# Tying the first running sum of each accumulator of the later modulations to its place in the source

## The chip, the cores and the metric

The kernel runs on one core of one Trainium2 chip. The metric is device time in microseconds (us), the median of repeated executions; lower is better. The engines are named as in the profile: PE (TensorE), DVE (VectorE), ACT (ScalarE), POOL (GpSimd) and SP, the engine that issues nearly all transfers (DMAs) from one queue, in the order in which they stand there.

## The reference

One layer of a streaming encoder: a prompt of 2048 tokens and a sample of 64, of width 1024. Scale, shift and gate of both halves of the layer come from the conditioning vectors c through one matrix, the six "modulations" of 1024 values each:

```python
def mlstm_chunk(carry, xs):
    C, n, m = carry
    q, k, v, ig, lf = xs
    ...
    a = wt * jnp.einsum('bhtd,bhsd->bhts', q, k)
    num = jnp.einsum('bhts,bhsd->bhtd', a, v) + g_inter[..., None] * jnp.einsum('bhvk,bhtk->bhtv', C, q)
```

The first half normalises x, projects it to a pooling mixer and to four heads of an mLSTM (queries, keys, values, gates; a matrix memory C carried from chunk to chunk), and projects back with a gated residual. The second half is a gated MLP of width 2816 with a causal convolution of width 3, again with a gated residual. All results are float32.

## The kernel before

The 2112 tokens are taken in four groups: 512, 512, 512 and 576. For each group the attention half runs on PE in this order: the projection of values and gates (`L1083`), then for each head the projections q, k, o (`L423`), between whose matmuls the head's mLSTM is laid (`L1173` to `L1265`), then pooling and the output projection. The MLP follows for all groups in stretches of hand-set order.

Weights. The matmuls of `L423` read units of 512 KB, `wt<-hl_kept` (`L355`), 12 matmuls to a unit (24 in the last group), two units to a projection. Six buffers hold units, and a unit's load is issued once PE has read the unit that held its buffer.

Gate chain. Between the gate projection and the first head stands a chain of some ten DVE and ACT steps on tiles of 4 rows, `L1118` to `L1186`: two scans (`L1136`, `L1144`), `R` (`L1159`, `L1161`) and `RHL` (`L1164`), which PE needs at `L1173` and `L1219`. `CL` and `GL` come from them; `kw` (`L1233`), `at` (`L1225`, `L1244`), the state updates `st` (`L1258`) and `nd` (`L1267`) are the mLSTM's own DVE steps.

Background work runs in generators which the main loop advances a step at a time:

- `ada(m, first)` makes modulation m, one per group (m = 2 in the first, then 3, 4, 5). It reads 16 blocks of `w_ada` of 128 x 512 (256 KB, `L188`), eight to each of two halves, into `raw` tiles, of which there are four (`RB`; m = 2 uses other tiles). For each block DVE adds to two accumulators: `tensor_scalar` at `L201` begins a half (k = 0), `scalar_tensor_tensor` at `L203` goes on (k = 1 to 7), each with the block times a column of `CA`, the conditioning. Three loads are issued ahead; the next one is issued behind the sums that free a buffer. Sums over partitions on PE (`L211`), a copy, transposes and the bias (`L221`) end it.
- `up_sums` loads `w_up` (`L843`), works on it on DVE (`L864` to `L868`) and stores `wsum` (`L853`) for the MLP; its steps keep the order of the source.
- The norm of the second half, in the last group, loads `mx<-x2d` (`L710`), works on DVE (`L698`) and ACT, stores `h2d` (`L718`).

The order on each engine is set by a tile scheduler, outside the hand-set stretches of the MLP: it may place an instruction earlier or later than the source has it, as long as data and buffers allow. `tc.keep_in_program_order(ins)` takes that freedom away for one instruction: it stays behind the instruction that stands ahead of it in the source on the same engine. It adds no semaphore and no work. Of all DMAs from SP at most eight are under way.

Of the kernel before, what the change touches and what calls it, by code (L numbers as in the profile page):

```python
# [12 lines left out]
ALU = mybir.AluOpType  # L13
# [46 lines left out]
def tile_layer(ctx: ExitStack, tc: tile.TileContext, xT, vecs, cst, rst, rowv, w_mod, w_ada, w_qkou, w_v, w_pool,  # L60
               w_out, w_up, w_down, st_C, st_pool, yT, o_pool, o_C, o_m, o_conv):
    nc = tc.nc
    act, dve, pool, pe = nc.scalar, nc.vector, nc.gpsimd, nc.tensor
# [19 lines left out]
    def m2_ps():  # L83
        return bank("m2")
# [9 lines left out]
    def scr():  # L94
        return sp.tile([P, TMAX], F32, tag="scr", name="scr")
# [56 lines left out]
    CA = cp.tile([P, KD, 2], F32, tag="CA", name="CA")  # L152
# [6 lines left out]
    def raw_tile():  # L159
        return wp.tile([P, WN], F32, tag="raw", name="raw", bufs=RB)  # L160
# [10 lines left out]
    def ada(m, first):  # L171


        todo = [(j, k) for j in range(2) for k in range(KD)]
        src = [w_ada[m - 2, k, :, j * 512:(j + 1) * 512] for j, k in todo]
        got = {}

        def load(i):
            if first:

                if i % 2 == 0 and i < len(todo):
                    w = a1.tile([P, 4, 256], F32, tag="w4", name="w4", bufs=5).rearrange("p (a b) c -> p a (b c)", a=2)
                    for d in range(2):
                        got[i + d] = w[:, d]
                        tc.keep_in_program_order(nc.sync.dma_start(out=w[:, d], in_=src[i + d]))
            elif i < len(todo):
                got[i] = raw_tile()[:, :512]
                nc.sync.dma_start(out=got[i], in_=src[i])  # L188
        lead = 4 if first else 3
        for i in range(lead):  # L190
            load(i)
        yield
        accs = []
        for i, (j, k) in enumerate(todo):
            if k == 0:
                acc = [a1.tile([P, 512], F32, tag="acc", name="acc", bufs=4) for _ in range(2)]
                accs += acc
            w = got.pop(i)
            for s in range(2):
                if k == 0:  # L200
                    dve.tensor_scalar(out=acc[s], in0=w, scalar1=CA[:, k, s:s + 1], scalar2=None, op0=ALU.mult)  # L201
                else:
                    dve.scalar_tensor_tensor(out=acc[s], in0=w, scalar=CA[:, k, s:s + 1], in1=acc[s],  # L203
                                             op0=ALU.mult, op1=ALU.add)
            load(i + lead)
            yield
        yield

        pt = m2_ps()
        for c, acc in enumerate(accs):  # L210
            pe.matmul(pt[32 * c:32 * c + 32, :], ones[:, 0:32], acc, start=True, stop=True)  # L211
        MR = scr()
        dve.tensor_copy(MR[:, :512], pt)
        yield
        yield
        pt = m2_ps()
        for n in range(4):
            pe.transpose(pt[:, n * P:(n + 1) * P], MR[:, n * P:(n + 1) * P], ident)
        for j in range(2):
            bia = V[:, V_BA + m * 8 + 4 * j:V_BA + m * 8 + 4 * j + 4]  # L220
            dve.tensor_tensor(out=MOD[:, m, 4 * j:4 * j + 4],  # L221
                              in0=pt.rearrange("p (n c t) -> p n c t", n=4, c=4)[:, :, 2 * j:2 * j + 2, 0],
                              in1=bia.unsqueeze(2).broadcast_to([P, 4, 2]), op=ALU.add)
        if m == 4:
            scale_cols(G2, V_G2, 4, 0, KD)
        yield

    def scale_cols(G, v0, m, k0, n):
        dve.scalar_tensor_tensor(out=G[:, k0:k0 + n], in0=MOD[:, m, k0:k0 + n], scalar=1.0,
                                 in1=V[:, v0 + k0:v0 + k0 + n].unsqueeze(2).broadcast_to([P, n, 2]),  # L230
                                 op0=ALU.add, op1=ALU.mult)
# [101 lines left out]
    class Unit:  # L333

        state = 0
        w = raw = None
# [494 lines left out]
    if True:  # L831
# [536 lines left out]
        for o in groups:  # L1368
# [3 lines left out]
            if o.g > 0:  # L1372
                bg[3].append(ada(2 + o.g, False))
                tick(3)
# [18 lines left out]
            if o.g == 0:  # L1393
                bg[3].append(ada(2, True))
# [505 lines left out]
```

## Time and profile before

| | |
|---|---|
| time, median of 3 runs | 2216.25 us (2215.57 to 2217.02) |
| the profiled execution | 2218.49 us |
| its span | 2216.7 us |
| mean granted PE clock | 0.995 |
| PE busy | 2191.5 us, 99% |
| DVE busy | 1570.1 us, 71% |
| ACT busy | 1004.3 us, 45% |
| DMA, whole span | 498.58 MB, 225 GB/s |

In the rows of the profile, `out<-in` are the program's names, `xcount` counts instructions that stand together, and a bracket holds the idle time before a row and what ended it. `SPq` is SP's queue of issues. The attention half ends near 806 us; groups 1, 2 and 3 begin their first head near 238, 424 and 613 us. The numbers behind names, as in `wt_4568`, tell tiles apart; where the profile leaves them out, the n-th issue of a kind in the trace is the n-th of its kind in the order.

### The profile page before, as it was taken

To read this page: it belongs to the slowest core of one execution; us is meant where nothing else is said; L and a number is where in the kernel's file an instruction comes from. 1 tells how busy PE (TensorE), PEld (TensorE's weight loads), DVE (VectorE), ACT (ScalarE), POOL (GpSimd) and SP (SyncE) were. 2 spreads that over 40 slices of the span, in tenths; PEclk is the share of its full clock that TensorE was granted. 3 is DMA by queue.
4 is the path that set the end of the run, shared out by engine and by line. 5 is a ranking of instruction groups with operands and counts; after the bars stand their busy time and mean duration, and the time that the engine had idled before them with its cause. 6 is when DMAs were issued, how large, how long until landed. Compare 5 with 4: busy or idle time off the path is not lost.

```text
span 2216.7 us, 38129 instructions
## 1 busy us (share of the span) xinstructions
PE 2191.5 (99%) x13798; PEld 2081.8 (94%) x13798; DVE 1570.1 (71%) x2917; ACT 1004.3 (45%) x1992; POOL 203.2 (9%) x481
## 2 busy tenths in 40 slices
PE   8999999999999999999999999999999999999998
PEld 6888888888899999999999999999999999999998
DVE  4877659577765768687858687777767685767474
ACT  3553334234343446464636454545445353445354
POOL 0010000001000100010100210000001210101012
PEclk9999999999999999999999999999999999999999
DMA  9978987997898695757656876556458565353442
GB/s 352 339 241 269 337 280 239 320 318 244 286 326 273 215 307 176 231 170 262 201 179 223 279 225 204 181 193 203 152 163 283 187 193 161 111 177 120 149 150 80
DMA packets 279357, 498.58 MB, mean 225 GB/s; under 512 B 25176, under 2 KB 105432, under 8 KB 279168
## 3 DMA queue, kind: packets, MB, share of 16 engines
q1 hardware_dynamic: 267392, 468.05, 64.6%
q10 hardware_dynamic: 11776, 28.09, 3.4%
q8 instruction: 109, 1.79, 0.3%
q14 instruction: 80, 0.66, 0.1%
HBM read 385.29 MB, written 110.75 MB: 224 GB/s over the span
## 4 chain that ended last, share of the span: by engine, by line
PE 91%; DMA 4%; DVE 2%; ACT 1%; issue 1%; SPq 1%; POOL 0%; POOLq 0%; DVEq 0%; ACTq 0%
PE mm L1488 37%; PE mm L423 23%; PE mm L1751 21%; PE mm L1083 3%; DMA wt<-wsum 1%; DMA raw<-w_down 1%; PE mm L1013 1%; PE m L1264 1%; PE m L1265 1%; DMA wt<-hl_kept 1%; PE m L1242 1%; PE m L1253 1%; PE m L1345 1%; PE p L1013 1%; DMA mx<-x2d 1%
## 5 line engine op out<-in xcount | busy, mean ns | idle before, releaser
L1488 PE MATMUL mm<-hx,wt 128*128 128x352 f32 x5544 | 886.1, 321 | 2.5 <-DVE ea L1540 2.4
L1488 PEld LDWEIGHTS mm<-hx,wt 128*128 128x128 f32 x5544 | 879.6, 188 | 4.5 <-ACT wt L366 2.5
L1751 PE MATMUL mm<-av,wt 128*128 128x352 f32 (+2 forms) x3168 | 509.7, 321 | 0.7 <-DVE av L1611 0.3
L1751 PEld LDWEIGHTS mm<-av,wt 128*128 128x128 f32 x3168 | 502.6, 188 | 4.2 <-ACT av L1603 1.2
L423 PE MATMUL mm<-hl,wt 128*128 128x512 f32 (+2 forms) x1920 | 397.6, 358 | 3.9 <-DMA wt<-hl_kept 2.7
L369 DVE TENSOR_TENSOR wt<-raw,wt 128x512 fp32r<-128x512 f32 (+3 forms) x494 | 307.1, 637 | 93.1 <-ACT wt L366 92.0
L366 ACT ACTIVATE wt<-raw 128x512 fp32r<-128x512 f32 (+3 forms) x494 | 271.7, 570 | 213.6 <-PE mm L1751 83.6
L423 PEld LDWEIGHTS mm<-hl,wt 128*128 128x128 f32 x1920 | 312.4, 188 | 52.1 <-issue 5.1
L1766 DVE SCALAR_TENSOR_TENSOR x<-mm,MOD,x 128x352 f32<-128x352 f32 (+4 forms) x224 | 106.5, 526 | 114.7 <-PE mm L1751 114.6
L423 PE MATMUL mm<-mx,wt 128*128 128x512 f32 (+1 forms) x960 | 186.7, 353 | 0.0
L423 PEld LDWEIGHTS mm<-mx,wt 128*128 128x128 f32 x960 | 158.7, 188 | 25.3 <-ACT mx L1347 1.1
L1476 DVE SCALAR_TENSOR_TENSOR tg<-eg,V,tg 128x704 f32<-128x704 f32 (+1 forms) x132 | 125.7, 952 | 47.9 <-ACT tg L1471 45.5
L369 DVE TENSOR_TENSOR wt<-wt 128x512 fp32r<-128x512 f32 x176 | 121.8, 693 | 53.1 <-ACT wt L366 52.7
L366 ACT ACTIVATE wt<-wt 128x512 fp32r<-128x512 f32 x176 | 110.2, 627 | 85.9 <-DMA wt<-wsum 74.3
L1476 DVE SCALAR_TENSOR_TENSOR ta<-ea,V,ta 128x704 f32<-128x704 f32 (+1 forms) x132 | 125.6, 952 | 8.5 <-ACT ta L1471 5.9
L1611 DVE TENSOR_TENSOR av<-tg,av 128x704 fp32r<-128x704 f32 (+4 forms) x112 | 62.1, 589 | 42.5 <-ACT av L1603 42.3
L1582 ACT ACTIVATE tg<-tg 128x704 f32<-128x704 f32 (+1 forms) x66 | 52.4, 794 | 77.7 <-DVE tg L1476 77.7
L1496 DVE TENSOR_TENSOR eg<-mm,u 128x352 f32<-128x352 f32 x154 | 70.2, 468 | 20.6 <-ACT u L1551 11.2
L203 DVE SCALAR_TENSOR_TENSOR acc<-raw,CA,acc 128x512 f32<-128x512 f32 x84 | 60.6, 748 | 32.7 <-DMA raw<-w_ada 32.6
L1536 ACT ACTIVATE u<-mm 128x352 f32<-128x352 f32 x66 | 30.4, 461 | 115.2 <-PE mm L1488 74.5
L1083 PE MATMUL mm<-wt,hl 128*128 128x256 f32 (+1 forms) x576 | 70.9, 282 | 0.0
L1083 PEld LDWEIGHTS mm<-wt,hl 128*128 128x128 f32 x576 | 69.2, 188 | 1.0 <-issue 0.6
(294 smaller groups left out, 1958.9 us busy)
## 6 DMA issues: line engine op xcount, KB each, us to landing
wt<-hl_kept SPq DMA_DIRECT2D x108, 512.0 KB, 5.9
raw<-w_up SPq DMA_DIRECT2D x198, 256.0 KB, 3.6
wt<-wsum SPq DMA_DIRECT2D x176, 256.0 KB, 4.1
wt<-wsplit SPq DMA_DIRECT2D x88, 512.0 KB, 4.1
raw<-w_down SPq DMA_DIRECT2D x96, 256.0 KB, 2.9
w<-w_up SPq DMA_DIRECT2D x88, 256.0 KB, 5.8
wsum<-w SPq DMA_DIRECT2D x44, 512.0 KB, 6.3
wsplit<-wt SPq DMA_DIRECT2D x44, 512.0 KB, 4.4
```

The source lines that it names most:

```text
L203: dve.scalar_tensor_tensor(out=acc[s], in0=w, scalar=CA[:, k, s:s + 1], in1=acc[s], op0=ALU.mult, op1=ALU.add)
L366: act.activation(u.w[:, 0, :u.n], u.raw[:, :u.n], AF.Copy)
L369: dve.tensor_tensor(out=u.w[:, 1, :u.n], in0=u.raw[:, :u.n], in1=u.w[:, 0, :u.n].bitcast(F32), op=ALU.subtract)
L423: pe.matmul(ps[bi][:, :hi - lo], U[:, a, k % 4 * P:(k % 4 + 1) * P], mv[k][:, b, lo:hi], start=(at == 0 and pi == 0), stop=(k == order[-1] ...
L1083: pe.matmul(ps[ti][:n, :cols], h[4 * kh + k4][:, b, lo:lo + n], U[:, a, k4 % 2 * cols:(k4 % 2 + 1) * cols], start=(kh == 0 and k4 == 0 and ...
L1476: dve.scalar_tensor_tensor(out=t[:, :E], in0=ext[:, j:j + E], scalar=wc(j, f), in1=t[:, :E], op0=ALU.mult, op1=ALU.add)
L1488: pe.matmul(ps[:, :FH], U[:, a, kc * P:(kc + 1) * P], Bo.at(nm, kc, b), start=(first and kc == 0 and pi == 0), stop=(kc == 3 and pi == 2), ...
L1496: dve.tensor_tensor(out=ext[:, d:d + b - a], in0=ps[:, a:b], in1=u[:, a:b], op=ALU.add)
L1582: act.activation(self.tg[:, :E], self.tg[:, :E], AF.Silu)
L1611: dve.tensor_tensor(out=cut(1), in0=self.of_tg(cut(0), a, b), in1=cut(0).bitcast(F32), op=ALU.subtract)
L1751: pe.matmul(ps[i][:, :hi - lo], U[:, a, k % 4 * P:(k % 4 + 1) * P], av[k](b, lo, hi), start=(k == 0 and (a, b) == PASSES[0]), stop=(k == n ...
L1766: dve.scalar_tensor_tensor(out=x3[n][:, a:b], in0=ps[i][:, a - lo:b - lo], scalar=gt2(n, s), in1=x3[n][:, a:b], op0=ALU.mult, op1=ALU.add)
```

## The change

Only the first sums at `L201` are touched: they are wrapped in `keep_in_program_order`. The statement takes one more line, so everything behind `L203` of before stands one line lower after (`L203` is now `L204`, `L355` is `L356`, `L1164` is `L1165`).

```diff
                 if k == 0:
-                    dve.tensor_scalar(out=acc[s], in0=w, scalar1=CA[:, k, s:s + 1], scalar2=None, op0=ALU.mult)
+                    tc.keep_in_program_order(dve.tensor_scalar(out=acc[s], in0=w, scalar1=CA[:, k, s:s + 1], scalar2=None,
+                                                               op0=ALU.mult))
                 else:
```

The number of matmuls, sums and loads stays. The later sums of an accumulator need its first one, and a load needs a free buffer, so both move with it.

DVE in group 2, the gate chain. `acc` are the accumulators of the modulation, `raw` the blocks of w_ada, `w4` the tiles of `up_sums`. Before:

```order
L1126 SCALAR_TENSOR_TENSOR scr_4336<-scr_4299 4x512
L203 SCALAR_TENSOR_TENSOR acc_4441<-raw_4465,CA_127,acc_4441 128x512
L203 SCALAR_TENSOR_TENSOR acc_4442<-raw_4465,CA_127,acc_4442 128x512
L1133 SCALAR_TENSOR_TENSOR scr_4299<-scr_4299,scr_4336 4x512
L203 SCALAR_TENSOR_TENSOR acc_4441<-raw_4475,CA_127,acc_4441 128x512
L1136 SCALAR_TENSOR_TENSOR scr_4393<-RST_145,scr_4299 4x512
L1144 SCALAR_TENSOR_TENSOR M_207<-scr_4299,M_207,scr_4298 4x512
L1148 TENSOR_TENSOR scr_4336<-scr_4298,scr_4393 4x512
L203 SCALAR_TENSOR_TENSOR acc_4442<-raw_4475,CA_127,acc_4442 128x512
L1153 TENSOR_TENSOR scr_4298<-scr_4393,M_207 4x512
```

And now:

```order
L1162 TENSOR_TENSOR R4_203<-scr_4336,scr_4298 4x512
L865 TENSOR_TENSOR w4_3828<-w4_3828 128x256
L1165 TENSOR_TENSOR RHL_205<-scr_4298,RHL_205 4x512
L866 TENSOR_TENSOR w4_3828<-w4_3828 128x256
L201 TENSOR_SCALAR acc_4441<-raw_4130,CA_127 128x512
L201 TENSOR_SCALAR acc_4442<-raw_4130,CA_127 128x512
L868 TENSOR_TENSOR w4_3828<-w4_3828 128x256
L204 SCALAR_TENSOR_TENSOR acc_4441<-raw_4132,CA_127,acc_4441 128x512
```

Before, the sums of the fifth and sixth block (`raw_4465`, `raw_4475`) stand within the chain, and those of the first four ahead of it. Now the first sums, and with them all others, stand behind `RHL`; the chain has no running sum in it. Ahead of `kw` of the first head stand the sums of ten blocks, where thirteen did.

SP in the same place. `wt` are weights of the first head: 4542 and 4568 belong to its third projection, 4601 and 4659 to the next head's first. Before:

```order
L355 DMA wt_4542<-hl_kept_128 128x2x512
L188 DMA raw_4558<-w_ada 128x512
L843 DMA w4_4565<-w_up 128x2x256
L853 DMA wsum_129<-w4_3828 512x1x256
L843 DMA w4_4565<-w_up 128x2x256
L355 DMA wt_4568<-hl_kept_128 128x2x512
L188 DMA raw_4578<-w_ada 128x512
L853 DMA wsum_129<-w4_4024 512x1x256
L188 DMA raw_4596<-w_ada 128x512
L355 DMA wt_4601<-hl_kept_128 128x2x512
```

Now, first the place where 4568 and 4601 stand, then that of 4659:

```order
L356 DMA wt_4542<-hl_kept_128 128x2x512
L356 DMA wt_4568<-hl_kept_128 128x2x512
L188 DMA raw_4465<-w_ada 128x512
L356 DMA wt_4601<-hl_kept_128 128x2x512
L188 DMA raw_4475<-w_ada 128x512
L188 DMA raw_4496<-w_ada 128x512
```

```order
L188 DMA raw_4578<-w_ada 128x512
L854 DMA wsum_129<-w4_4024 512x1x256
L188 DMA raw_4596<-w_ada 128x512
L844 DMA w4_4633<-w_up 128x2x256 x2
L188 DMA raw_4654<-w_ada 128x512
L356 DMA wt_4659<-hl_kept_128 128x2x512
```

Of the loads of the fifth to the twelfth block (`raw_4465` to `raw_4596`), all eight stood ahead of `wt_4601`, and now one does. `wt_4659` keeps its place behind `raw_4654`, the thirteenth block, whose buffer was that of the ninth, `raw_4537`; the loads from the fifth block on now all stand behind the first sums, and so behind the gate chain.

SP in group 3, where a unit has 24 matmuls. `wt_6515` and `wt_6553` are the first head's third projection, `wt_6601` is the next head's first unit. Before:

```order
L355 DMA wt_6515<-hl_kept_128 128x2x512
L853 DMA wsum_129<-w4_5666 512x1x256
L355 DMA wt_6553<-hl_kept_128 128x2x512
L355 DMA wt_6601<-hl_kept_128 128x2x512
L843 DMA w4_6631<-w_up 128x2x256 x2
```

Now:

```order
L356 DMA wt_6553<-hl_kept_128 128x2x512
L188 DMA raw_6414<-w_ada 128x512
L188 DMA raw_6446<-w_ada 128x512
L844 DMA w4_6456<-w_up 128x2x256 x2
L188 DMA raw_6475<-w_ada 128x512
L854 DMA wsum_129<-w4_5666 512x1x256
L188 DMA raw_6508<-w_ada 128x512
L188 DMA raw_6540<-w_ada 128x512
L844 DMA w4_6550<-w_up 128x2x256 x2
L188 DMA raw_6569<-w_ada 128x512
L854 DMA wsum_129<-w4_5879 512x1x256
L188 DMA raw_6594<-w_ada 128x512
```

The row behind these is `wt_6601`, and one more w_ada load, `raw_6398`, stands ahead of `wt_6553`. Before, all eight stood ahead of `wt_6330`, the first head's first unit. In this group the first DVE steps of the norm (`L698`) also stand behind more running sums than before, and of its six steps on reloaded tiles that stood ahead of the second head's state updates, two still do; a third stands between the updates.

In group 1 the running sums move in the same way, to behind `RHL`, and three w_ada loads now stand ahead of `wt_2692`, the second head's first unit. In group 0 (m = 2) the two first sums move a few rows.

## The prediction

> **What bounds the kernel now.** I read the page's first rows and its chain first, then the windows around the slices in which TensorE (PE) is short of 100%, then the timelines and the issues of loads there.
>
> ```profile
> PE 2191.5 (99%) x13798; PEld 2081.8 (94%) x13798; DVE 1570.1 (71%) x2917; ACT 1004.3 (45%) x1992; POOL 203.2 (9%) x481
> PE 91%; DMA 4%; DVE 2%; ACT 1%; issue 1%; SPq 1%; POOL 0%; POOLq 0%; DVEq 0%; ACTq 0%
> 430.00:440.00 10.00, 7.52 (x35) 5.57 (x33) 6.82 (x15) 2.81 (x6) 0.00 (x0) 1.00 1.02 332
> 440.00:450.00 10.00, 9.82 (x50) 8.68 (x51) 7.78 (x18) 2.36 (x10) 0.00 (x0) 0.83 1.06 386
> 450.00:670.00 220.00, 220.00 (x1347) 192.78 (x1346) 159.89 (x352) 88.98 (x222) 13.43 (x19) 1.00 0.87 290
> 670.00:680.00 10.00, 8.39 (x62) 7.45 (x61) 6.24 (x23) 3.73 (x16) 0.66 (x1) 1.00 1.01 346
> ```
>
> PE is the bound. A microsecond of VectorE (DVE, 71%) costs nothing unless PE ends up waiting for it. The columns of a window's row are its length, the busy time of PE, PE's loads, DVE, ACT and POOL, then PE's granted clock. In the stretch the change touches, PE loses time in two places: 2.66 us at 430 to 450 (the first two windows), where its clock also drops, and 1.61 us at 670 to 680. The 220 us between hold no idle time.
>
> ```profile
> 437.40:440.90 3.50, 1.58 (x7) 1.04 (x7) 2.40 (x6) 0.60 (x1) 0.00 (x0) 1.00 1.05 342
> 440.90:444.30 3.40, 3.40 (x14) 2.92 (x14) 2.14 (x4) 1.14 (x4) 0.00 (x0) 0.55 1.03 386
> 444.30:447.70 3.40, 3.40 (x22) 3.06 (x21) 3.40 (x8) 0.00 (x0) 0.00 (x0) 0.95 1.07 395
> 434.99 2.35 PE L423 MATMUL mm<-hl,wt 128*128 128x512 f32 x9 [0.74 <-DMA wt<-hl_kept]
> 440.18 2.01 PE L423 MATMUL mm<-hl,wt 128*128 128x512 f32 x6 [1.92 <-DMA wt<-hl_kept]
> 446.33 1.63 PE L423 MATMUL mm<-hl,wt 128*128 128x512 f32 x6
> 674.22 0.49 PE L1264 MATMUL m<-st,q 128*128 128x129 f32 x2 [1.61 <-DVE st L1258]
> ```
>
> The rows at 434.99 and 440.18 wait for weights: wt_4568 and wt_4601 of group 2. The clock then stands at 0.55 for 3.40 us and at 0.95 for as long, which loses 0.45 x 3.40 + 0.05 x 3.40 = 1.70 us. So group 2 pays 0.74 + 1.92 + 1.70 = 4.36 us. Why the weights are late is in the queues:
>
> ```profile
> 432.80 0.15 SPq L188
> 433.04 7.00 DMA wt<-hl_kept
> 415.40 0.63 ACT L1130 ACTIVATE scr<-scr 4x512 f32<-4x512 f32 x1
> 416.82 1.42 DVE L203 SCALAR_TENSOR_TENSOR acc<-raw,CA,acc 128x512 f32<-128x512 f32 x2 [3.47 <-DMA raw<-w_ada]
> 418.15 0.67 DVE L1133 SCALAR_TENSOR_TENSOR scr<-scr 4x512 f32<-4x512 f32 x1
> 425.87 0.68 DVE L1164 TENSOR_TENSOR RHL<-scr,RHL 4x512 fp32r<-4x512 f32 x1
> 430.04 0.94 SPq L355 DMA_DIRECT2D wt<-hl_kept  x1
> 433.04 0.88 SPq L355 DMA_DIRECT2D wt<-hl_kept  x1
> 434.01 1.84 SPq L843 DMA_DIRECT2D w<-w_up  x2
> 436.58 0.53 SPq L355 DMA_DIRECT2D wt<-hl_kept  x1
> ```
>
> The chain of waits (first two rows) goes from a w_ada load on the SP queue, held by DVE's running sums, to the weights behind it. On DVE two running sums wait 3.47 us for w_ada data at 416.82, and the gate chain (L1133 to L1164), whose input ACT had ready at 416.03, starts at 418.15. The three hl_kept issues are wt_4568, wt_4601 and wt_4659.
>
> **The change part by part.** No instruction is added: what moves is when the sums run and, through their four raw buffers, when SP may issue. The prices:
>
> ```profile
> L203 DVE SCALAR_TENSOR_TENSOR acc<-raw,CA,acc 128x512 f32<-128x512 f32 x84 | 60.6, 748 | 32.7 <-DMA raw<-w_ada 32.6
> 426.58 0.76 DVE L865 TENSOR_TENSOR w<-w 128x256 f32<-128x256 f32 x2
> 427.26 0.42 DVE L867 TENSOR_TENSOR w<-w 128x256 f32<-128x256 f32 x1
> 431.25 0.88 DVE L201 TENSOR_SCALAR acc<-raw,CA 128x512 f32<-128x512 f32 x2
> 432.04 1.41 DVE L203 SCALAR_TENSOR_TENSOR acc<-raw,CA,acc 128x512 f32<-128x512 f32 x2
> 433.37 0.13 DVE L1143 COPY M<-M 4x1 f32<-4x1 f32 x1
> wt<-hl_kept SPq DMA_DIRECT2D x14, 512.0 KB, 7.0
> raw<-w_ada SPq DMA_DIRECT2D x12, 256.0 KB, 6.3
> wt<-hl_kept SPq DMA_DIRECT2D x3, 528.0 KB, 5.5
> ```
>
> By starts, an up-sum step takes 0.34 us (427.26 less 426.58, for two), a first sum 0.40, a later sum 0.67. The issues of 395 to 450 land after 7.0 and 6.3 us; the last row, from 570 to 640, is shorter. The 32.6 us that later sums spend waiting for w_ada cost nothing as such.
>
> *Group 2, gain.* The gate chain starts at 416.1 instead of 418.15 and has two sums and one up-sum step fewer ahead of L1164: that ends at 426.55 - 2.05 - 2 x 0.67 - 0.34 = 422.8. One up-sum step and two first sums later, at 424.0, the first w_ada load goes out. wt_4568 now stands ahead of that load and wt_4601 directly behind it, issued by 424.7 and landed by 431.7 even at 7.0 us. PE wants them at 434.99 - 0.74 = 434.25 and, without the first wait, 440.18 - 1.92 - 0.74 = 437.5. Both waits go, and with them I take the dip: -4.36 us. What is late next is wt_4659.
>
> *Group 2, price.* It stands behind raw_4654, whose buffer comes free with the second of the second half's first sums. From 424.0 DVE has ahead of that: 14 later sums (9.4), 12 up-sum steps (4.1), two first sums (0.8) and two small copies (0.2), so 438.5 with no wait. A load goes out as a buffer comes free and is wanted three steps later (six sums and about five up-sum steps, 5.7 us), 0.6 us before it has landed; over the first half that adds some 1 us: 439.5. wt_4659 then goes at 440.0 (bounds 439.2 and 440.5), not 436.58. PE wants it three matmuls after 446.33, at 447.0 in the trace, so at 442.7 once 4.36 us are gone. Landing after 6.7 us (between the two medians of that window) gives 446.7: a stall of 4.0 us. Some of it may show as a wait for kw (L1233), which stands two more sums behind. As two waits of 2.66 us together brought a dip, so should this: +1.7. Net +4.0 + 1.7 - 4.36 = +1.3. Bounds: 439.2 and 5.5 us, no dip: 2.0 - 4.36 = -2.4; 440.5 and 7.0, two dips: 4.8 + 3.4 - 4.36 = +3.8.
>
> *Group 3.*
>
> ```profile
> 602.83 1.41 DVE L203 SCALAR_TENSOR_TENSOR acc<-raw,CA,acc 128x512 f32<-128x512 f32 x2 [1.72 <-DMA raw<-w_ada]
> 604.17 0.92 DVE L1122 TENSOR_SCALAR scr<-m,RV 4x512 f32<-4x512 f32 x2
> 616.32 0.75 DVE L1164 TENSOR_TENSOR RHL<-scr,RHL 4x576 fp32r<-4x576 f32 x1
> 619.18 1.61 SPq L355 DMA_DIRECT2D wt<-hl_kept  x2
> 632.44 1.85 PE L423 MATMUL mm<-hl,wt 128*128 128x256 f32 x12
> 673.31 0.58 DVE L698 SCALAR_TENSOR_TENSOR mx<-mx,G,mx 128x352 f32<-128x352 f32 x1 [1.77 <-DMA mx<-x2d]
> ```
>
> Without the pair at 602.83 the chain starts some 1.35 us sooner, and L1164 ends at 617.07 - 1.35 = 615.7. The first pair of sums is done at 616.9. Now wt_6601, which went with wt_6553 at 619.18 to 620.8 before, stands behind eight w_ada loads. The last of them needs 14 later sums and 10 up-sum steps more: 9.4 + 3.4 = 12.8, plus 0.5 for landing, so 630.2. wt_6601 goes at 630.5 (629.7 to 631) and lands after 6.0 us (5.5 to 7.0): 636.5. The 632.44 row has six matmuls of the unit before and six that want wt_6601: 633.3. Stall 3.2 us (1.9 to 4.7), and a dip of 1.7 (0 to 1.7). The 1.61 us at 672.6 is DVE at L698, waiting for a norm reload that stands ahead of the state update st. Six such L698 stand ahead of st before, two now, with a third behind the first two updates; so -1.6 (0 to -1.6). Net 3.2 + 1.7 - 1.6 = +3.3 (0.3 to 6.4).
>
> *Group 1.*
>
> ```profile
> 241.36 0.53 SPq L355 DMA_DIRECT2D wt<-hl_kept  x1
> 254.81 1.40 PE L423 MATMUL mm<-hl,wt 128*128 128x512 f32 x5
> ```
>
> wt_2692, issued at 241.36, is wanted three matmuls behind 254.81, at 255.5. By the same walk it goes at about 246.5, behind three w_ada loads, and lands by 253.5: covered by 2 us. Were that cover gone, each us late is a us; +0.3 (0 to 1.5), which stands for a wait for kw. Group 0's modulation moves a few rows at most: 0.
>
> [...]
>
> Sum: 1.3 + 3.3 + 0.3 = +4.9 us. The profiled run took 2218.49 us (span 2216.7), 2.24 above the median of 2216.25, so by the median 2216.25 + 4.9 = 2221.2.
>
> **The rivals.**
>
> *Late loads still land in time (faster).* Place: wt_4659 and wt_6601. If DVE catches up, wt_4659 issued by 442.7 - 7.0 = 435.7 and wt_6601 by 633.3 - 6.0 = 627.3 cost nothing: -4.36 - 1.6 = -6.0, 2210.3. For it: DVE idles 3.47 us at 416.82 for data, and would now find its first four loads landed. Against: 14.5 and 12.8 us of sums stand between. Halfway cases give -2. Chance 0.20.
>
> *Stalls in all groups.* Once PE has waited, later units (wt_4726, wt_4749) stand behind further w_ada loads, each some 1.5 us late, group 1 loses 1.0 at kw and a dip of 1.7: 4.9 + 3.0 + 2.7 = +10.6, about 2227. For it: the same queue pattern in three groups. Against: six weight buffers, and group 1 had no wait. Chance 0.20.
>
> *The tie does nothing that counts.* The sums land in DVE's idle time and loads go as before: 2216. The order contradicts it, since wt_6601 passes from three rows behind wt_6515 to fourteen; chance 0.05.
>
> **How the numbers follow.** My forecast has 0.55. Its own range, -2.1 to +11.7 by the bounds, lies mostly between +1 and +9. A measurement of this kernel tells about 0.2% (4.4 us) from no change. Of the 0.55, 0.32 lie above that and 0.23 within. The faster rival gives 0.13 faster and 0.07 within; stalls in all groups 0.20 slower; nothing 0.05 within. Faster 0.13, same 0.35, slower 0.52. The range takes in most of the faster rival and ends at the second's 2227: 2211.5 to 2227.
>
> **What would show it.** Right: no wait for wt_4568 and wt_4601, but one of 2 to 5 us for wt_4659 near 443 to 447 with a dip behind; a wait near 633 to 637 for hl_kept; RHL of group 2 done near 423; nothing over 0.5 us near 672. Wrong: PE busy 10.00 in all slices from 420 to 680 (the faster rival), or waits at kw and in group 1 (the second).

## The result, and the profile after

| | before | after |
|---|---|---|
| time, median of 6 runs | 2216.64 us (2214.25 to 2218.91) | 2229.21 us (2224.88 to 2230.16) |
| the profiled execution | 2218.49 us | 2224.88 us |
| its span | 2216.7 us | 2223.1 us |

The ratio is 1.0049, with a 95% interval of 1.0040 to 1.0059: slower by 10.9 us (8.9 to 13.1); the medians alone lie 12.6 us apart. The forecast was +4.9 and a range that ended at 2227. The profiled execution after is the shortest of its six, that of before is 1.9 us over its median; this will matter. One run of a later experiment, the repetition of the second half's tie, stood at a granted clock of 0.655 and took 3084 us; it is left out of that comparison.

Windows of after, with the columns of the prediction's windows, and then PE's timeline of after, of which only rows with a wait are shown:

```profile
430.00:440.00 10.00, 10.00 (x55) 8.43 (x54) 9.97 (x23) 3.95 (x10) 0.00 (x0) 1.00 1.00 325
440.00:450.00 10.00, 6.57 (x30) 5.41 (x30) 6.33 (x15) 0.93 (x5) 0.00 (x0) 0.83 0.98 350
450.00:460.00 10.00, 8.44 (x41) 6.04 (x40) 7.89 (x18) 5.50 (x17) 1.46 (x1) 1.00 0.84 266
630.00:640.00 10.00, 8.80 (x67) 8.52 (x66) 8.45 (x23) 4.08 (x13) 0.00 (x0) 1.00 1.01 344
640.00:650.00 10.00, 8.76 (x56) 8.48 (x57) 6.39 (x14) 1.33 (x5) 0.00 (x0) 0.83 1.04 380
670.00:680.00 10.00, 10.00 (x80) 8.93 (x72) 7.73 (x20) 5.30 (x14) 0.00 (x0) 1.00 1.06 376
```

```profile
261.45 0.49 PE L1266 MATMUL m<-va,at 128*128 128x129 f32 x2 [0.63 <-DVE at L1245]
446.19 1.64 PE L424 MATMUL mm<-hl,wt 128*128 128x512 f32 x3 [3.43 <-DMA wt<-hl_kept]
456.93 0.66 PE L1296 MATMUL m<-ident,nd 128*128 128x128 f32 x4 [1.56 <-DVE nd L1285]
471.19 0.49 PE L1254 MATMUL m<-va,kw 128*128 128x129 f32 x2 [0.57 <-DVE kw L1234]
641.24 3.18 PE L424 MATMUL mm<-hl,wt 128*128 128x256 f32 x12 [2.44 <-DMA wt<-hl_kept]
```

The old losses are gone: nothing at 430 to 440, where wt_4568 and wt_4601 were late, and nothing at 670 to 680. In their place PE waits 3.43 us for wt_4659 and 2.44 us for wt_6601, a clock dip behind each (0.83 of a 10 us window, 1.7 us), and 0.63, 1.56 and 0.57 us for steps of DVE. How it comes about stands in three views of after: DVE's timeline, SP's timeline with its issues, and a stretch of the chain of waits (start, length, what held it):

```profile
415.99 0.68 DVE L1134 SCALAR_TENSOR_TENSOR scr<-scr 4x512 f32<-4x512 f32 x1 [2.70 <-ACT scr L1131]
422.29 0.68 DVE L1165 TENSOR_TENSOR RHL<-scr,RHL 4x512 fp32r<-4x512 f32 x1
437.76 0.88 DVE L201 TENSOR_SCALAR acc<-raw,CA 128x512 f32<-128x512 f32 x2
439.88 0.69 DVE L1234 TENSOR_TENSOR kw<-m,CL 128x512 f32<-128x512 f32 x1
```

```profile
424.67 0.59 SPq L356 DMA_DIRECT2D wt<-hl_kept  x1
437.34 1.33 SPq L844 DMA_DIRECT2D w<-w_up  x2
438.78 0.54 SPq L188 DMA_DIRECT2D raw<-w_ada  x1
439.73 0.53 SPq L356 DMA_DIRECT2D wt<-hl_kept  x1
```

```profile
439.20 0.53 PE m L1243 x5
439.73 6.42 DMA wt<-hl_kept
446.19 1.22 PE mm L424 x2
```

The gate chain runs from 415.99 to 422.97 without a sum in it, and wt_4601 goes at 424.67, not 433.04. DVE then has the whole first half's sums to do; the second half's first sums end at 438.64, raw_4654 goes at 438.78 and wt_4659 behind it, at 439.73. In the chain PE's work leads straight into that load, because the last thing that SP waits for ahead of it is a step of PE (SP's waits of 424 to 448 us: in total, times, longest):

```profile
SPq L356 <- PE m L1243: 0.7, 1, 0.7
```

That wait is short and comes behind raw_4654. What holds the load up to there is the raw buffer that the sums free; the experiment with these loads on another queue shows it.

### The profile page after: what moved, and what is told of

It reads as the page before. It is cut to its first block, busy times and chain, and to the rows that moved or that the text cites. A ratio compares the mean times of both kernels' runs of the same rounds, so it can differ in the third digit from the quotient of the medians.

```text
span 2223.1 us, 38156 instructions
## 1 busy us (share of the span) xinstructions
PE 2194.2 (99%) x13798; PEld 2083.7 (94%) x13798; DVE 1569.6 (71%) x2917; ACT 1005.9 (45%) x1992; POOL 200.5 (9%) x481
## 4 chain that ended last, share of the span: by engine, by line
PE 91%; DMA 4%; DVE 2%; ACT 1%; issue 1%; SPq 0%; POOL 0%; POOLq 0%; DVEq 0%; ACTq 0%
PE mm L1489 37%; PE mm L424 23%; PE mm L1752 21%; PE mm L1084 3%; DMA wt<-hl_kept 1%; DMA wt<-wsum 1%; PE m L1266 1%; PE mm L1014 1%; PE m L1265 1%; PE m L1254 1%; PE m L1243 1%; PE m L1346 1%; PE p L1014 1%; PE m L929 0%; PE m L1296 0%
## 5 line engine op out<-in xcount | busy, mean ns | idle before, releaser
L1472 ACT ACTIVATE tg<-eg,V 128x704 f32<-128x704 f32 (+1 forms) x66 | 63.9, 968 | 9.6 <-DVE eg L1497 9.6
```

Source lines behind the costliest of these rows:

```text
L1472: act.activation(t[:, :E], ext[:, 2:2 + E], AF.Identity, scale=wc(2, f), bias=V[:, V_BC + f:V_BC + f + 1])
```

## The experiments

Theory A: PE loses time where a weight unit stands in SP's queue behind w_ada loads that wait for sums, and by clock dips behind such waits; all of it lies in groups 1 to 3. In a window, PE's idle time is the length less PE's busy time, and a dip is what the clock lacks of 1.00 times the length (by the clock's two digits the same dip reads 1.7 or 1.8, 3.3 or 3.4 us).

**Where the time goes: the same kernel again, and the tie in one group at a time.** The edit for a single group (here m = 4):

```diff
-                    tc.keep_in_program_order(dve.tensor_scalar(...))
+                    ins = dve.tensor_scalar(...)
+                    if m == 4:
+                        tc.keep_in_program_order(ins)
```

> The changed kernel once more, for a second profile. Theory A (new waits of PE in groups 1 to 3, each of the longer ones followed by a clock dip): the time is again 10 to 13 us above before; where the profiled execution is near the median of 2229, the 4 to 6 us by which it is above the first profile (2224.9) are further dips or longer waits between 240 and 690 us. Rival B (a drift elsewhere): those 4 to 6 us lie behind 806 us, in the MLP.

Measured: 2228.0 us (2226.97 to 2233.81), ratio 1.0059 (1.0047 to 1.0072). Its profiled execution is at the median; its windows:

```profile
430.00:460.00 30.00, 25.27 (x123) 20.00 (x122) 24.42 (x55) 10.90 (x32) 1.46 (x1) 0.94 0.95 321
630.00:650.00 20.00, 16.44 (x108) 15.93 (x107) 13.20 (x32) 5.41 (x18) 0.00 (x0) 0.83 0.99 348
```

Group 2 loses as in the first profile (4.73 us of waits). Group 3 loses 3.56 us for wt_6601 and a dip of 0.17 x 20 = 3.4 us where it had 2.44 and 1.7 before: 2.8 of the 3.1 us between the two executions. Rival B falls.

> Only the modulation of group 1 (m = 3) is tied. Theory A: group 1 has one wait of 0.6 us in the trace of the full change and no dip, so +0.5 to +2 us over before; group 2 keeps its old waits for wt_4568 and wt_4601. Rival B, a loss that comes from any tie wherever it stands: +4 us, a third of the whole.

2215.7 us, ratio 0.9997 (0.9988 to 1.0006): no change, where theory A expected 0.5 to 2 us.

> Only the modulation of group 2 (m = 4) is tied. Theory A: 3.43 + 1.56 + 0.57 us of waits and a dip of 1.7 take the place of 2.66 us and a dip of 1.7, so +2.9 us by the profile, +3 to +6 by the median, with the wait for wt_4659 in the trace. Rival B: +4 us without these waits.

2221.71 us, ratio 1.0028 (1.0017 to 1.0039): +5.3 us from its before of 2216.42. Its windows show the wait for wt_4659 and the one for nd (4.71 us) and a dip:

```profile
430.00:460.00 30.00, 25.29 (x122) 20.03 (x122) 24.44 (x56) 10.49 (x32) 1.45 (x1) 0.94 0.97 321
```

> Only the modulation of group 3 (m = 5) is tied. Theory A: 2.44 us for wt_6601 and a dip of 1.7 come, 1.61 us at 672 go: +2.5 us by the profile, +2 to +6 by the median; group 2 as before. Rival B: +4 us without these waits. The three ties should add up to the whole within 2 us by theory A.

2219.55 us, ratio 1.0015 (1.0007 to 1.0024): +3.1 us. Group 3 waits 3.13 us, with a dip of 1.8, and the 1.61 us at 670 to 680 are gone. Group 2 is as in the kernel before, and here it has its old waits (2.06 us) without any dip. Its windows:

```profile
430.00:460.00 30.00, 27.94 (x143) 22.65 (x142) 24.27 (x55) 11.31 (x30) 1.46 (x1) 1.00 0.98 337
630.00:650.00 20.00, 16.87 (x115) 15.97 (x116) 14.47 (x33) 4.92 (x19) 0.00 (x0) 0.91 0.93 315
```

**Queue or bandwidth: the loads on another queue.** The edit, on the changed kernel and on the one before:

```diff
                 got[i] = raw_tile()[:, :512]
-                nc.sync.dma_start(out=got[i], in_=src[i])
+                nc.gpsimd.dma_start(out=got[i], in_=src[i])
```

> All ties kept, but the w_ada loads of the later modulations are issued from POOL's queue instead of SP's. Theory A (the weights are late because they stand behind w_ada loads in SP's queue, each of which waits for running sums): no wait of PE for hl_kept in groups 2 and 3 and no dip there; what is left are short waits for DVE (kw, nd), 0 to 3 us; 2210 to 2218. Rival C (the weights are late because the transfers crowd the same DMA engines, busy at 1.0 there): the waits for hl_kept stay at 1.5 us or more each, 2222 to 2229.

2216.18 us, ratio 1.0000 (0.9991 to 1.0009). PE's waits between 60 and 850 us (in total, times, longest):

```profile
PE m L1254 <- DVE kw L1234: 2.6, 2, 2.2
PE m L1186 <- ACT CL L1180: 1.1, 1, 1.1
PE mm L424 <- ACT wt L367: 1.0, 1, 1.0
PE mm L424 <- DMA wt<-hl_kept: 0.7, 1, 0.7
```

With the same bytes and the same ties, the waits for wt_4659 and wt_6601 are gone; 0.7 us for hl_kept are left, near 690. wt_4659 goes 11 us earlier than in the profile after, and takes longer to land than its 6.42 us there (SP's timeline, then the issues of 428.5 to 428.7, with the KB and the time to landing):

```profile
428.57 0.63 SPq L356 DMA_DIRECT2D wt<-hl_kept  x1
wt<-hl_kept SPq DMA_DIRECT2D x1, 512.0 KB, 8.4
```

The queue is the cause, not the crowd of transfers: rival C falls. But the time only falls to that of the kernel before: PE reaches kw 2.18 us too early, since kw stands behind ten blocks of sums on DVE, and a dip of 1.7 us follows (0.83 from 440 to 450 us). What the weights no longer cost, DVE's order costs in part.

> The kernel before with the w_ada loads on POOL's queue, no tie. Theory A: the old waits for wt_4568 and wt_4601 (2.66 us, at times with a dip) shrink or go, since no w_ada load stands ahead of them: 2211 to 2217, at most 1 us from the tied kernel on POOL except for what the gate chain's delay costs. Rival C: the waits of 2.66 us stay, 2215 to 2219.

2233.23 us, ratio 1.0078 (1.0064 to 1.0092): both expectations missed. Two of the longest of PE's waits between 60 and 850 in this kernel, and a row of its DVE timeline in group 1:

```profile
PE m L491 <- DVE scr L485: 7.7, 3, 4.4
PE m L1265 <- DVE at L1244: 3.0, 1, 3.0
```

```profile
231.52 0.75 DVE L203 SCALAR_TENSOR_TENSOR acc<-raw,CA,acc 128x512 f32<-128x512 f32 x1 [3.49 <-DMA raw<-w_ada]
```

There is no wait for hl_kept here either. But without the tie the sums stand ahead of the copy at L485 and of the gate chain, wait there for data, and hold PE. Why the data comes that late by POOL's queue I did not follow up. With these loads on POOL the tie is worth -17 us; with them on SP it costs 11.

**Which half.** The tie for j = 0 or for j = 1 alone.

> Only the first sums of the first half (j = 0) are tied, in all later modulations. Theory A: this tie moves all sums behind the gate chain and keeps wt_4659 and wt_6601 behind the same w_ada loads, so nearly the whole loss is here: +8 to +12 us, with waits of 2 to 4 us for hl_kept in groups 2 and 3. Rival D (the loss is from the second half's first sums being held behind other work ahead of kw): +0 to +4 us.

2225.17 us, ratio 1.0042 (1.0028 to 1.0056): +8.4. The longest of PE's waits between 60 and 850 us:

```profile
PE m L1255 <- DVE kw L1235: 3.9, 2, 2.2
PE mm L425 <- DMA wt<-hl_kept: 2.5, 1, 2.5
PE m L1297 <- DVE nd L1286: 1.6, 1, 1.6
```

Half right: the tie of the first half has most of the loss, but in group 2 it is kw that PE waits for (2.16 us, until 443.80; the other 1.70 us are for kw in group 1), and PE comes to wt_4659 at 446.85 without a wait for it: the wait for kw covers that load.

> Only the first sums of the second half (j = 1) are tied. The first half stays within the gate chain, and wt_4659, wt_6601 and wt_6674 stand ahead of the second half's w_ada loads. Theory A: the old waits for wt_4568 and wt_4601 stay, no new ones come: 2214 to 2218. Rival D: +4 to +10 us.

2214.53 us, ratio 0.9992 (0.9983 to 1.0001). In this order wt_4659 and wt_6601 stand ahead of the second half's w_ada loads. PE's rows with a wait, 405 to 480 us; this profile has no dip between 60 and 860 us:

```profile
438.88 1.63 PE L425 MATMUL mm<-hl,wt 128*128 128x512 f32 x6 [1.03 <-DMA wt<-hl_kept]
452.01 2.34 PE L425 MATMUL mm<-hl,wt 128*128 128x512 f32 x9 [0.32 <-DMA wt<-hl_kept]
456.32 5.77 PE L425 MATMUL mm<-hl,wt 128*128 128x512 f32 x24 [0.83 <-DMA wt<-hl_kept]
```

Rival D falls. The waits of 0.32 and 0.83 us are for wt_4749 and the unit behind it, which theory A did not have.

> The tie of the second half alone once more, to narrow its interval: 2214.5 before, so 1 to 3 us under the kernel before. Theory A: the profile has under 4 us of PE idle behind 60 us and hardly a dip. If its gain was chance, it comes within 1 us of before.

The repetition gave 0.9994 (0.9985 to 1.0003); by the medians it lies 0.1 us under its before (2215.73 and 2215.85). Its profile waits 4.5 us for hl_kept, where under 4 us of idle time were expected, in four waits of 0.7 to 1.5 us, and has no dip between 60 and 860 us. Both intervals reach 1, so a gain is not shown; no version here is shown to beat the kernel before.

**Do the parts add up?** By the medians the single ties give -0.7 + 5.3 + 3.1 = 7.7 us, the whole 11.6 to 12.6. By the ratios it is 8.9 us for 10.9 and 13.1, and each ratio is good to some 2 to 3 us.

> Ties in groups 1 to 3 but not in group 0 (m = 2), whose tie moves only a few rows on DVE. The single ties of groups 1, 2 and 3 gave -0.7, +5.3 and +3.1 us, 7.7 together, where the whole gives 11.6 to 12.6. Theory A (local waits and dips): 7 to 12 us, and the waits of groups 2 and 3 as in the whole. Rival E (group 0's tie has a share that its few rows don't show): not over 9 us.

2226.26 us, ratio 1.0043 (1.0029 to 1.0057): 10.4 us by the medians, 9.5 (6.4 to 12.6) by the ratio. The interval leaves room for rival E's 9 us, but the traces do not: in both profiles of the changed kernel PE has no wait of 0.3 us or more and no dip between 65 and 255 us, so group 0 has no loss to give.

> Ties in groups 2 and 3 alone. Theory A: 5.3 + 3.1 = 8.4 us, 7 to 10. Rival F (group 1's tie, nothing by itself, shifts the phase of later groups and so adds 3 to 4 us): this one at 8 while ties in groups 1 to 3 give 12.

2227.61 us, ratio 1.0046 (1.0033 to 1.0059), +11.8 from its before of 2215.85 by the medians, 10.2 (7.3 to 13.1) by the ratio. The difference of the medians lies above what both theories had, but theory A's 7 to 10 is inside the interval, so it is not shown that groups 2 and 3 cost more together than apart. Rival F falls: group 2 waits as long without group 1's tie (5.96 us) as with it (5.30 to 6.02). Its windows:

```profile
430.00:460.00 30.00, 24.60 (x117) 19.43 (x115) 23.05 (x53) 9.89 (x30) 1.46 (x1) 0.89 0.94 314
630.00:650.00 20.00, 17.31 (x121) 16.71 (x120) 14.41 (x34) 5.40 (x18) 0.00 (x0) 0.91 1.01 356
```

The dip in group 2 is 0.11 x 30 = 3.3 us, where the tie of m = 4 alone had 1.8; the wait for wt_4659 is 3.85 us. By group, with both ties in place:

| profile | group 2: waits, dip | group 3: waits, dip |
|---|---|---|
| after | 5.56, 1.8 | 2.44, 1.8 |
| again | 5.30, 1.8 | 3.56, 3.4 |
| m = 3, 4, 5 | 6.02, 3.3 | 3.64, 3.4 |
| m = 4, 5 | 5.96, 3.3 | 2.69, 1.8 |
| mean | 5.7, 2.6 | 3.1, 2.6 |
| a tie alone | 5.28, 1.8 (m = 4) | 3.13, 1.8 (m = 5) |

(waits of 430 to 480 and of 630 to 650 us). So by these profiles the waits are 0.4 us longer with both ties, and the dips 1.6 us. These are few profiles of a quantity that changes from execution to execution. In this table the dips of 3.3 and 3.4 us stand behind waits of 3.56 to 3.90 us for a weight unit, those of 1.8 behind waits of 2.44 to 3.43; how much of the 1.6 us the ties themselves bring is open.

**The wait at L1296.** The last edit, on the changed kernel:

```diff
-                    pe.transpose(ph[:, c0:c0 + n], nd[:n, ti, 0:128], ident[:n, :n])
+                    tc.keep_in_program_order(pe.transpose(ph[:, c0:c0 + n], nd[:n, ti, 0:128], ident[:n, :n]))
```

> The changed kernel with one more tie: the PE transposes of nd (L1296) too, which puts those of group 2's first head back behind nine more matmuls of the next projection, as they stand before the change; the queue of SP stays. Theory A (the 1.56 us at L1296 come from these transposes having moved ahead on PE, not from a slower DVE): that wait goes, the waits for wt_4659 and wt_6601 stay, and the time falls by 1 to 2 us from the changed kernel's 2228 to 2229, if wt_4749 lands in time. Rival G (nd itself is late by the running sums): the wait stays at 1 us or more in the later place.

2225.45 us, ratio 1.0043 (1.0026 to 1.0060). The wait for nd is gone, and the next thing is late in its place, wt_4749, as PE's timeline shows:

```profile
446.44 1.65 PE L424 MATMUL mm<-hl,wt 128*128 128x512 f32 x3 [3.19 <-DMA wt<-hl_kept]
457.20 2.33 PE L424 MATMUL mm<-hl,wt 128*128 128x512 f32 x9 [1.68 <-DMA wt<-hl_kept]
```

Rival G falls, nd was ready for a later place. But 1.56 us turned into 1.68 us, so the expected 1 to 2 us did not come from there; whether the 2.5 us by which its median is under that of the repetition are real, the intervals don't tell.

## Why the prediction was wrong

The direction and the mechanism were right, the size was not: +10.9 us for +4.9.

- *Group 2's gain.* The waits for wt_4568 and wt_4601 went, 2.66 us, and the gate chain ended at 422.97 for a forecast of 422.8. The -1.70 us for their dip is the first step that failed. In two later profiles in which group 2 still had the old order, it kept such waits and had no dip: 2.69 us with the tie of m = 3, 2.06 with m = 5. The longest single wait was 1.46 and 1.18 us there, and 1.92 in the profile of before, the shortest wait with a dip behind it in all the profiles between 60 and 850 us. The profile of before was an execution 2.24 us above the median of its three runs, which is about such a dip. I took the change from that execution's own losses and applied it to a median that most likely did not have the dip; that -1.70 was 0 in most executions is argued from these three profiles, not counted.
- *wt_4659.* Issued at 439.73 (forecast 440.0), landed after 6.42 us (6.7), a wait of 3.43 us (4.0; 3.18 to 3.90 in other profiles with this wait). This step held.
- *What I did not price.* The wait of 1.56 us at L1296 and 0.57 at the second head's kw. The first is a move on PE, whose order I did not go through: the transposes of nd moved ahead by nine matmuls. The last experiment shows that without it wt_4749 is 1.68 us late, which I had as part of a rival ("each some 1.5 us late") and at nothing in the sum. Either way some 2 us were missing.
- *Group 3.* PE waited 2.42 to 3.64 us for wt_6601 (forecast 3.2), the 1.61 us at 672 went. In the profile after the load went 4.3 us later than forecast (634.78 for 630.5), but PE also came to it 5.5 us later (638.80 for 633.3). The dip was 1.8 or 3.4 us for 1.7. Alone +3.1 for +3.3.
- *Group 1.* Waits of 0.63, 0.46 and 0.72 us in the three profiles with every tie, none of 0.3 us or more in that with the ties of groups 1 to 3, and no dip; the tie alone 0.9997: the 0.3 held.

With the measured means the sum comes out: group 2 is 5.7 + 2.6 - 2.66 = +5.6, group 3 is 3.1 + 2.6 - 1.6 = +4.1, group 1 +0.3: 10.0 for 10.9 measured. Of the 5.1 us that were missing from 4.9, 1.7 are the dip that was not there to gain, 1.7 the waits behind wt_4659 that were not priced (5.7 for 4.0), and 1.8 the dips that were longer than the 1.7 taken for each, less 0.1 for group 3's wait.

The rival "stalls in all groups" named the size, +10.6, but by another way: of its 2.7 us in group 1 at most 0.72 came, and wt_4749 was late only where nd was not. That its number came near is luck. The faster rival fell at the place it named, since wt_4659 went 4 us after the point from which it decides.

## What to carry to other kernels

Here a load that waited for DVE to free its buffer held the weights behind it in SP's queue: wt_4659 went at 439.73 us, directly behind raw_4654, and at 428.57 once the w_ada loads went by POOL's queue. So when work is moved later on an engine, look up which weights stand behind the loads that need its buffers, and cost them one after the other until PE is no longer early, since the wait that you remove can uncover the next (nd's 1.56 us, then 1.68 for wt_4749). Before a loss in the profile is booked as a gain, compare that execution's time with the median: a loss that only some executions have is no gain for the others. And one edit can change sign with the queue: in this kernel the tie costs 11 us with the loads on SP and saves 17 with them on POOL.

## What the runs showed of the hardware

Behind some of PE's waits the traces' record of the granted clock has a slow stretch. Between 60 and 2195 us the profile before has one, from 441.25 us on, and that after has two, from 446.23 and 640.79 us; each is 3.41 us long at 0.50, which is the dip of 1.7 us. The last 7.35 us of the span of before and the last 5.34 of that of after stood at 0.50 too. Within each of the two profiles these starts lie whole multiples of 3.4133 us apart: 441.25 and 2209.35 in that of before by 518 of them, 446.23, 640.79 and 2217.75 in that of after by 57 and 462. Counted in such steps from the start of the span they leave 0.93 us in the profile before and 2.50 us in that after.

The 14 profiles have 19 dips between 60 and 850 us. Each stands behind a single wait of PE of 1.92 us or more; behind a shorter one there is none (the longest is 1.81 us, for the copy at L485 in the kernel before with its loads on POOL). Of the 21 waits of 1.92 us or more, two had no dip behind them: the 2.16 us for kw with the tie of the first half, and 2.0 us for st at L1266 with the tie of m = 3. The dips behind the waits of 3.56, 3.64, 3.85 and 3.90 us were of 3.3 or 3.4 us, the others of 1.7, that behind the longest wait, 4.41 us in the kernel before with its loads on POOL, among them. In the columns of the prediction's windows, first before (1.92 us idle, then a dip), then the tie of m = 3 (1.85 us idle in a stretch as long, and no dip), then the ties of m = 3, 4, 5, where 2.19 us of the wait of 3.90 lie ahead of the slow stretch and 1.71 in it, and the stretch is twice as long:

```profile
437.83:441.25 3.42, 1.50 (x7) 0.91 (x6) 2.26 (x5) 0.60 (x1) 0.00 (x0) 1.00 1.03 338
441.25:444.66 3.41, 3.41 (x15) 3.02 (x14) 2.50 (x4) 1.14 (x4) 0.00 (x0) 0.50 1.05 393
```

```profile
670.07:673.48 3.41, 1.56 (x12) 1.56 (x13) 2.32 (x8) 1.52 (x5) 0.00 (x0) 1.00 1.02 350
673.48:676.89 3.41, 3.41 (x26) 2.90 (x25) 2.21 (x9) 1.90 (x11) 0.00 (x0) 1.00 0.81 300
```

```profile
440.94:444.35 3.41, 1.22 (x8) 0.89 (x6) 3.41 (x9) 0.00 (x0) 0.00 (x0) 1.00 0.97 294
444.35:447.76 3.41, 1.70 (x5) 1.41 (x6) 0.25 (x1) 0.00 (x0) 0.00 (x0) 0.50 1.06 393
447.76:451.17 3.41, 3.41 (x12) 2.95 (x12) 1.62 (x4) 1.25 (x6) 0.00 (x0) 0.50 0.66 238
```

So behind a wait of some 2 us the profiles show a dip of 1.7 us or none: kw's 2.18 us with the loads on POOL had one, kw's 2.16 us with the tie of the first half had none. What decides between the two is not shown. The lengths are those of these waits, with PE's ends as the profile models them.
